# The within-chunk inverses of a chunked DeltaNet scan: stored transposes and joined 128-row products in place of transposes and 64-row products

## The chip, the cores and the metric

The kernel runs on one core of a Trainium2 chip. The metric is the device time of one execution in microseconds (us). The profile's engine names are used: PE is the matrix engine, PEld its weight loads, DVE the vector engine, ACT the scalar engine, POOL the GpSimd engine, SP the engine that issues most DMAs.

## The reference

One layer of a hybrid trunk over 2048 latent tokens and 256 context tokens of width 1024. A combined input projection feeds two token mixers: a bidirectional chunked gated DeltaNet (4 heads, key and value width 128, chunks of 64) and a windowed attention. Both are gated, projected, merged and projected again. The change touches the DeltaNet alone:

```python
a_mat = jnp.where(strict, einsum('nbhik,nbhjk->nbhij', kb, kc) * decay, 0.0)
t_mat = triangular_solve(a_mat, eye, lower=True, unit_diagonal=True)   # 64 x 64, one per chunk and head
u = einsum('nbhij,nbhjv->nbhiv', t_mat, vc * bc)
w = einsum('nbhij,nbhjk->nbhik', t_mat, kb * exp(gc))
...
v_new = u_n - w_n @ s                                  # one step of the scan over chunks
s_new = s * exp(gl_n) + kd_n.T @ v_new
o = qd_n @ s + qk_n @ v_new
...
o = o_f + rev(o_b)                                     # the same on the reversed sequence
```

## The kernel before, in words

The kernel works on blocks of 128 tokens, that is two of the reference's chunks: 2 context blocks and 16 latent ones, NC = 18. A block's 128x128 unit-triangular inverse is made of two 64x64 inverses on its diagonal and one off-diagonal 64x64 piece, which is minus (inverse) x (off-diagonal of the matrix) x (inverse).

Stages in order. First the norms, the state projection, the qkv projection with the short convolution; `finish` (from L591) forms the 128x128 key products of each block and `spill_blocks` (from L583) stores their diagonal 64x64 blocks in `Nsp` and the off-diagonal block in `offsp`. Then `base` (from L727) inverts the 64x64 blocks, 128 of them at a time with one block in each partition, by 62 pairs of DVE instructions (L758, L760): it runs twice, first for 8 chunks of each direction (si = 0), then for 8 more (si = 1), and stores the inverses in `Xset`. `base4` (from L775) does the last 2 chunks of each direction in another layout, as a generator whose pieces are placed among the steps of the scan; it stores `X4sp` in quarters. While `base` runs, PE does the gate projections (`gates`, `rest_run`, from L823: rps, L535 to L537 as recorded inside `fm_dense`).

Then the scan: 18 steps, each with one block forwards and one backwards. `chain` (from L1094) carries the state: ksps (L1109), vps (L1115), sps (L1127) on PE, x (L1102) on POOL, L1111, L1118 and L1133 on DVE, v2 (L1123) on ACT. `output` forms aps (L1151) and ops (L1162). `merge` (from L999) builds the two 128x128 inverses `mw` (forward, transposed, as vps needs it as its left operand) and `mx` (backward) for the next step: it loads the 64x64 inverses into zeroed tiles, transposes them on PE (L1027, L1029), copies (L1034, L1035), multiplies with the off-diagonal block (L1037 forward, L1039 backward; `in_step` issues the two directions alternately on different 64x64 parts of the PE array), evicts (L1041, L1042), multiplies again (L1044, L1046) and evicts into the off-diagonal quarter (L1048, L1049). `finalize` normalizes a block's output and transposes it (fps, L1078).

A planner orders each engine's instructions ahead of time from a simulated run, with priorities: the scan has the higher priority, and the gate projections of the other tokens (30 runs of 24 products before the attention is called for, 18 more behind it) fill PE between its steps. The attention follows (sc, L926 and on), and then the projections. At run time each engine, and SP's queue of DMAs, goes through its list in that fixed order.

Of the kernel before, what the change touches and what calls it, by code (L numbers as in the profile page):

```python
# [20 lines left out]
H = 4  # L21
# [19 lines left out]
def _hybrid(ctx, tc, nc, V, S, G, T, ins, out, dbg, upto):  # L41
# [61 lines left out]
    Xsp = [{}, {}]  # L103
    X4sp = dscr("X4sp", [2, 2, 4, 8, 64, 16])
    gsp = dscr("gsp", [1, D])
    osp = many("osp", NB, [128, H * 128])
    zasp = many("zasp", 4, [4, 128, 512])
# [623 lines left out]
    def base(si, npool, pool, fr, bk):  # L731


        n = 8 * len(fr)
        h1 = max(32, n)
        N = npool.tile([128, 64, 64], F32, name="N")
        nb = npool.tile([128, 64], F32, name="nb")
        if n < h1:
            G.memset(N[0:h1], 0.0)
            G.memset(nb[0:h1], 0.0)  # L740
        for d, chunks in ((0, fr), (1, bk)):
            for i0, c, k in runs(chunks):
# [24 lines left out]
        V.memset(A.rearrange("p r c -> p (r c)")[:, ::65], 1.0)  # L767
        for d, chunks in ((0, fr), (1, bk)):
            p0 = d * h1
            dma(Xset[d][si].rearrange("c h b r j -> (c h b) (r j)"), N[p0:p0 + n].rearrange("p r j -> p (r j)"))  # L770
            for ci, c in enumerate(chunks):
                Xsp[d][c] = Xset[d][si][ci]
        yield 1

    def base4(fr, bk):  # L775
# [8 lines left out]
        G.memset(nc_, 1.0)  # L784
        for d, chunks in ((0, fr), (1, bk)):
            c, p0 = chunks[0], d * 16
            dma((nc_, nb)[d][p0:p0 + 16], brT[c:c + 2, d * 4:d * 4 + 4].rearrange("c h (b t) -> c (h b) t", b=2))
            dma(N[p0:p0 + 16], Nsp[d][c:c + 2].rearrange("c h b r i -> (c h b) r i"))
        G.memset(X, 0.0)
# [18 lines left out]
        for d, chunks in ((0, fr), (1, bk)):  # L808
            for ci, c in enumerate(chunks):
                for q in range(4):  # L810
                    p0 = q * 32 + d * 16 + ci * 8
                    dma(X4sp[d, ci, q], X[p0:p0 + 8])
        yield

    def rest(ev, m, by_act):
# [43 lines left out]
    with tc.tile_pool(name="gate", bufs=1, reuse_waits="tile") as gp:  # L859
        gates(list(range(24)), (2, 3), behind(4, mod_gate(gp, ones)), by_act=True)  # L860
    LAST = (LAT(14, 15), LAT(0, 1))
    for si, (fr, bk, np_) in enumerate((([0, 1] + LAT(*range(0, 6)), [0, 1] + LAT(*range(10, 16)), bs),
                                        (LAT(*range(6, 14)), LAT(*range(2, 10)), bs2))):
        with tc.issue_after(last_conv[0].ins):
            for _ in base(si, np_, bs2, fr, bk):
                pass
    last_base = base4(*LAST)
    next(last_base)
    mem("r1a")
# [117 lines left out]
            weighted(n, kv, qs[n], pr.pop(i))  # L987


    def in_step(products):  # L990

        first = None
        for h in range(H):
            for p in products:
                with tc.issue_after(first.ins) if first else nullcontext():
                    i = p(h)
                first = i

    def merge(pool, cs):  # L999

        hs = range(H)
        Xs, offs, tp = [], [], []
        for d, c in enumerate(cs):
            X = pool.tile([128, H, 128], F32, name=f"mx{d}", bufs=2)
            G.memset(X, 0.0)
            if c in LAST[d]:
                x4 = pool.tile([128, 4, H, 16], F32, name="x4")
                for b in range(2):  # L1010
                    bs_ = slice(b * 64, b * 64 + 64)
                    for q in range(4):
                        dma(x4[bs_, q], X4sp[d, LAST[d].index(c), q, b::2].rearrange("h r s -> r h s"))
                    G.tensor_copy(X[bs_, :, bs_].rearrange("p h (s q) -> p h s q", q=4),
                                  x4[bs_].rearrange("p q h s -> p h s q"))
            else:
                for b in range(2):
                    dma(X[b * 64:b * 64 + 64, :, b * 64:b * 64 + 64], Xsp[d][c][:, b].rearrange("h r c -> r h c"))
            off = pool.tile([128, H, 64], F32, name=f"moff{d}", bufs=2)
            dma(off[64:128], offsp[d][c])  # L1020
            Xs.append(X)
            offs.append(off)
        for d in range(2):
            tps = psum(f"mg{d}", [128, H, 128], name="mtp")
            for h in hs:
                if d == 0:
                    T.transpose(tps[:, h], Xs[0][:, h], ident)  # L1027
                else:
                    T.transpose(tps[:, h, 64:128], Xs[1][64:128, h], ident[64:128, 64:128])  # L1029
            tp.append(tps)  # L1030
        brb = [br[:, c, d * 4:d * 4 + 4].unsqueeze(2).to_broadcast([128, H, 64]) for d, c in enumerate(cs)]
        y0, y1 = offs[0], pool.tile([128, H, 64], F32, name="my1")
        W, X = pool.tile([128, H, 128], F32, name="mw", bufs=2), Xs[1]
        S.copy(W, tp[0])  # L1034
        V.tensor_tensor(y1[64:128], tp[1][64:128, :, 64:128], brb[1][64:128], op=ALU.mult)  # L1035
        yps = [psum(f"mg{d}", [128, H, 128], name="myp") for d in range(2)]
        in_step([lambda h: T.matmul(yps[0][0:64, h, 0:64], lhsT=offs[0][64:128, h], rhs=W[64:128, h, 64:128],  # L1037
                                    start=True, stop=True),
                 lambda h: T.matmul(yps[1][64:128, h, 0:64], lhsT=offs[1][64:128, h], rhs=y1[64:128, h],  # L1039
                                    start=True, stop=True)])  # L1040
        V.tensor_tensor(y0[0:64], yps[0][0:64, :, 0:64], brb[0][0:64], op=ALU.mult)  # L1041
        S.copy(y1[0:64], yps[1][64:128, :, 0:64])  # L1042
        eps_ = [psum(f"mg{d}", [128, H, 128], name="mep") for d in range(2)]
        in_step([lambda h: T.matmul(eps_[0][0:64, h, 0:64], lhsT=Xs[0][0:64, h, 0:64], rhs=y0[0:64, h],  # L1044
                                    start=True, stop=True),
                 lambda h: T.matmul(eps_[1][64:128, h, 0:64], lhsT=y1[0:64, h], rhs=X[0:64, h, 0:64],  # L1046
                                    start=True, stop=True)])
        S.activation(W[0:64, :, 64:128], eps_[0][0:64, :, 0:64], AF.Copy, scale=-1.0)  # L1048
        S.activation(X[64:128, :, 0:64], eps_[1][64:128, :, 0:64], AF.Copy, scale=-1.0)  # L1049
        return W, X  # L1050

    def scan_consts(pool):
# [30 lines left out]
    def scan(pool, pool2, cs, after):  # L1083
# [83 lines left out]
                dma(osp[b], oa.rearrange("p h d -> p (h d)"))  # L1167
                seen.add(b)

        W = merge(pool, [orders[d][0] for d in range(2)])  # L1170
        for st in range(NC):
            r = [chain(d, st, W[d]) for d in range(2)]
            ready = [finalize(pool2, b, oa, cs, d) for b, oa, d in late]
            late.clear()
            if st + 1 < NC:
                W = merge(pool, [orders[d][st + 1] for d in range(2)])
            for rest in ready:
                rest()
            for d in range(2):
# [422 lines left out]
```

## Time and profile before

| what | value |
|---|---|
| three runs, us | 1989.85, 1990.79, 1998.35; median 1990.79 |
| the profiled execution, us | 1992.9, its span 1991.2 |
| mean granted clock of PE | 0.989 |
| PE, PEld busy | 1917.4 us (96%), 1605.6 us (81%) |
| DVE, ACT, POOL busy | 1502.1 us (75%), 802.6 us (40%), 692.1 us (35%) |
| DMA traffic | 333.12 MB, 387703 packets |

In the views, a row of a group gives line, engine, operation, destination and sources by tile name, shapes and count, then the busy time in us and the mean of one in ns, then the engine's idle time before it. A row of the timeline gives the start in us, the duration in us of the merged instructions, and what they are. Matmuls overlap in their pipeline, so what one costs PE is read from start to start, not from its duration. A float32 product appears as two matmul instructions. A row of stretches gives the stretch, its length, and then each engine's busy time with the number of instructions, the granted clock, the DMA engines' busy share and GB/s.

### The profile page before, as it was taken

The numbers are of one execution on the slowest core, as the hardware profiler recorded it, in microseconds if no ns is written. First come the engines' busy times: TensorE is split into PE (matmuls) and PEld (weight loads), VectorE is DVE, ScalarE is ACT, GpSimd is POOL, SyncE is SP. The second block draws the span as 40 slices with busy tenths as digits, with TensorE's granted clock in tenths as the row PEclk, the third lists the DMA queues.
The fourth block names the chain that finished last, engine by engine and source line by source line (L and its number), as shares of the span: only waits on it lengthen the run. The fifth ranks groups of instructions, "written<-read, shape, count | busy, mean of one in ns | idle before, by whom it ended". The sixth has DMA issues, their size and how long they took to land. (4 is left out here: it accounts for less than half of the span.)

```text
span 1991.2 us, 32088 instructions
## 1 busy us (share of the span) xinstructions
PE 1917.4 (96%) x10947; PEld 1605.6 (81%) x10947; DVE 1502.1 (75%) x2869; ACT 802.6 (40%) x1994; POOL 692.1 (35%) x768
## 2 busy tenths in 40 slices
PE   7999999989999999999999999999989999999998
PEld 4888888779998787877888888788778887877786
DVE  6979766668776999999677776536686878747888
ACT  5755545554443323111222233225665656532221
POOL 2742211235542202004222234323555443420675
PEclk9999999999999999999999999999999999999999
DMA  7552226765547633528977877674455655455454
GB/s 263 173 142 87 91 89 161 195 157 175 151 134 196 170 106 116 145 89 237 230 232 225 240 212 207 178 216 146 143 176 171 185 161 164 119 173 190 141 169 135
DMA packets 387703, 333.12 MB, mean 167 GB/s; under 512 B 83992, under 2 KB 307536, under 8 KB 386900
## 3 DMA queue, kind: packets, MB, share of 16 engines
q1 hardware_dynamic: 352244, 288.60, 50.1%
q10 hardware_dynamic: 35296, 42.48, 6.1%
q8 instruction: 87, 1.43, 0.3%
q14 instruction: 76, 0.62, 0.1%
HBM read 220.28 MB, written 109.13 MB: 165 GB/s over the span
## 5 line engine op out<-in xcount | busy, mean ns | idle before, releaser
L535 PE MATMUL rps<-hh,wh 128*128 128x512 f32 x768 | 309.3, 403 | 3.7 <-DVE rt L829 2.5
L537 PE MATMUL rps<-hh,wl 128*128 128x512 f32 x768 | 307.6, 401 | 0.0
L536 PE MATMUL rps<-hl,wh 128*128 128x512 f32 x768 | 307.5, 400 | 0.0
L574 DVE SCALAR_TENSOR_TENSOR cacc<-y,cw,cacc 128x512 f32<-128x512 f32 (+1 forms) x224 | 164.0, 752 | 22.2 <-ACT cacc L572 18.3
L535 PEld LDWEIGHTS rps<-hh,wh 128*128 128x128 f32 x768 | 145.3, 189 | 39.4 <-DVE rt L829 3.3
L535 PE MATMUL lps<-hh,wh 128*128 128x512 f32 (+1 forms) x448 | 171.8, 384 | 0.3 <-ACT y L645 0.3
L536 PE MATMUL lps<-hl,wh 128*128 128x512 f32 (+1 forms) x448 | 171.5, 383 | 0.0
L537 PEld LDWEIGHTS rps<-hh,wl 128*128 128x128 f32 x768 | 145.2, 189 | 32.6
L536 PEld LDWEIGHTS rps<-hl,wh 128*128 128x128 f32 x768 | 145.5, 189 | 31.9
L537 PE MATMUL lps<-hh,wl 128*128 128x512 f32 (+1 forms) x448 | 171.0, 382 | 0.0
L961 DVE TENSOR_TENSOR pl<-pt,ph 128x512 fp32r<-128x512 f32 x156 | 105.4, 685 | 42.9 <-ACT ph L959 42.1
L959 ACT CAST ph<-pt 128x512 fp32r<-128x512 f32 x156 | 90.2, 585 | 110.2 <-PE pt L957 77.0
L827 ACT ACTIVATE rt<-rps 128x512 f32<-128x512 f32 x96 | 57.3, 597 | 185.0 <-PE rps L537 169.0
L933 DVE CUSTOM_DVE_ANT_0 pr<-sc,band,sk 128x640 f32<-128x640 f32 (+1 forms) x128 | 106.6, 862 | 32.1 <-PE sc L929 16.2
L943 POOL TENSOR_SCALAR pr<-pr,sm 128x640 f32<-128x640 f32 (+1 forms) x128 | 99.7, 802 | 56.5 <-DVE sm L941 39.3
L760 DVE TENSOR_TENSOR N<-N,btmp 128x62 f32<-128x62 f32 (+30 forms) x124 | 116.7, 941 | 3.0
L758 DVE TENSOR_TENSOR btmp<-N 128x62 f32<-128x62 f32 (+30 forms) x124 | 116.4, 939 | 3.1
L935 ACT ACTIVATE pr<-pr,sm 128x640 f32<-128x640 f32 (+1 forms) x128 | 104.0, 815 | 20.5 <-DVE sm L933 20.4
L246 DVE TENSOR_TENSOR wl<-wr,wh 128x512 fp32r<-128x512 f32 x120 | 92.4, 783 | 24.4 <-POOL wh L245 22.1
L1247 PE MATMUL pps<-yh,wph 128*128 128x512 f32 x256 | 105.6, 414 | 4.7 <-DVE tb L1258 2.5
L245 POOL TENSOR_SCALAR wh<-wr 128x512 fp32r<-128x512 f32 x72 | 48.8, 692 | 169.8 <-PE lps L536 97.1
L1248 PE MATMUL pps<-yl,wph 128*128 128x512 f32 x256 | 101.8, 399 | 0.0
(378 smaller groups left out, 5025.4 us busy)
## 6 DMA issues: line engine op xcount, KB each, us to landing
wr<-in_w_in_dram SPq DMA_DIRECT2D x120, 256.0 KB
kw<-Ksp SPq DMA_DIRECT2D x28, 384.0 KB
x<-vsp SPq DMA_DIRECT2D x36, 256.0 KB
k<-ksp SPq DMA_DIRECT2D x34, 256.0 KB
kT<-kTsp SPq DMA_DIRECT2D x34, 256.0 KB
wm<-in_w_mod_dram SPq DMA_DIRECT2D x16, 512.0 KB
xt<-in_x_dram SPq DMA_DIRECT2D x16, 512.0 KB
dtl<-Dsp SPq DMA_DIRECT2D x32, 256.0 KB
```

Of the source, the lines that this page charges most:

```text
L535: T.matmul(ps, lhsT=wh[:, k], rhs=xh[:, k], start=k == 0, stop=False)
L536: T.matmul(ps, lhsT=wh[:, k], rhs=xl[:, k], start=False, stop=False)
L537: T.matmul(ps, lhsT=wl[:, k], rhs=xh[:, k], start=False, stop=k == kt - 1)
L574: V.scalar_tensor_tensor(a, y[:, t:t + n], cw[:, m, t:t + 1], a, op0=ALU.mult, op1=ALU.add)
L758: V.tensor_tensor(tv, A[:, m + 1:, m].unsqueeze(2).to_broadcast([h1 + n, r, m]), A[:, m, 0:m].unsqueeze(1).to_broadcast([h1 + n, r, m]), o ...
L760: V.tensor_tensor(A[:, m + 1:, 0:m], A[:, m + 1:, 0:m], tv, op=ALU.add)
L933: V.tensor_tensor_reduce(s_, ps[:, o:768], band[:, b0:b0 + W + 256], -0.125, sk[:, 1, hd:hd + 1], ALU.add, ALU.min, sm[:, h, 1:2])
L935: S.activation(s_, s_, AF.Exp, scale=-1.0, bias=sm[:, h, 1:2], accum_out=sm[:, h, 2:3])
L943: G.tensor_scalar(p[:, h, :W + 256], p[:, h, :W + 256], sm[:, h, 3:4], 1.0, op0=ALU.mult, op1=ALU.mult)
L961: V.tensor_tensor(pl, pt, f32(ph), op=ALU.subtract)
L1247: T.matmul(ps, lhsT=wh[:, k, ms], rhs=hs[k], start=k == 0, stop=False)
L1248: T.matmul(ps, lhsT=wh[:, k, ms], rhs=ls[k], start=False, stop=False)
```

## The change

`base` also copies each set of inverses transposed (four ACT copies of a quarter each, each followed by two stores to the new scratch `XTset`), and `base4` likewise (one ACT copy, 16 stores to `XT4sp`). `spill_blocks` stores the forward off-diagonal block from the untransposed product instead of the transposed one. `merge` loads the forward inverses transposed, places the off-diagonal blocks of the two directions in the two off-diagonal quarters of one 128x128 tile `off` that was zeroed once, and forms both directions' products in one product of 128 rows a head. The right-hand factors are stacked: `r1` is scaled by br on POOL before the first product, `r2` is copied by ACT. The transposes, DVE's two instructions and `in_step` are gone. The tiles are zeroed once (`merge_tiles`) and not in each step. `off` and the intermediate `z` have one buffer.

```diff
@@ spill_blocks
-        dma(offsp[d][c0:c0 + nn, :, h].rearrange("c r i -> r c i"), t[64:128, :, 0:64])
+        if d:
+            dma(offsp[1][c0:c0 + nn, :, h].rearrange("c r i -> r c i"), t[64:128, :, 0:64])
+            dma(offsp[0][c0:c0 + nn, :, h].rearrange("c r i -> r c i"), t[0:64, :, 64:128])
@@ base, after the store to Xset
+        for q in range(4):
+            xt = (pool.tile([128, 1376], F32, name="btmp") if npool is pool else
+                  xtp.tile([128, 1024], F32, name="xt"))[0:h1 + n, 0:1024].rearrange("p (j r) -> p j r", r=64)
+            S.copy(xt, A[:, :, q * 16:q * 16 + 16].rearrange("p r j -> p j r"))
+            for d in range(2):
+                dma(XTset[d][si].rearrange("c h b j r -> (c h b) j r")[:, q * 16:q * 16 + 16], xt[d * h1:d * h1 + n])
@@ base4, after the stores to X4sp
+        S.copy(N[:, 0:16], X.rearrange("p r s -> p s r"))
+        for d, chunks in ((0, fr), (1, bk)):
+            for ci, c in enumerate(chunks):
+                for q in range(4):
+                    p0 = q * 32 + d * 16 + ci * 8
+                    dma(XT4sp[d][ci].rearrange("h b (s q) r -> (h b) s q r", q=4)[:, :, q], N[p0:p0 + 8, 0:16])
@@ merge: the new body (the old one is in the listing above)
+        lo_, hi_ = slice(0, 64), slice(64, 128)
+        W, X, off, z = tiles[0][st % 2], tiles[1][st % 2], tiles[2], tiles[3]
+        r1 = pool.tile([128, H, 64], F32, name="mr1", bufs=2)
+        r2 = pool.tile([128, H, 64], F32, name="mr2", bufs=2)
...
+        for b, bs_ in enumerate((lo_, hi_)):
+            dma(W[bs_, :, bs_], blk(XTsp[0][cs[0]][:, b]))
+            if cs[1] in LAST[1]:
+                quarters(X[bs_, :, bs_], 1, b)
+            else:
+                dma(X[bs_, :, bs_], blk(Xsp[1][cs[1]][:, b]))
+        if cs[0] in LAST[0]:
+            quarters(r1[lo_], 0, 0)
+        else:
+            dma(r1[lo_], blk(Xsp[0][cs[0]][:, 0]))
+        dma(r1[hi_], blk(XTsp[1][cs[1]][:, 1]))
+        for d, (rows, cols) in enumerate(((lo_, hi_), (hi_, lo_))):
+            dma(off[rows, :, cols], offsp[d][cs[d]])
+            G.tensor_tensor(r1[rows], r1[rows], br[rows, cs[d], d * 4:d * 4 + 4].unsqueeze(2).to_broadcast([64, H, 64]),
+                            op=ALU.mult)
+        S.copy(r2[hi_], W[hi_, :, hi_])
+        S.copy(r2[lo_], X[lo_, :, lo_])
+        zps = psum("mg0", [128, H, 64], name="mzp")
         for h in range(H):
+            T.matmul(zps[:, h], lhsT=off[:, h], rhs=r1[:, h], start=True, stop=True)
+        S.copy(z[hi_, :, lo_], zps[hi_])
+        S.copy(z[lo_, :, hi_], zps[lo_])
+        eps_ = psum("mg1", [128, H, 64], name="mep")
+        for h in range(H):
+            T.matmul(eps_[:, h], lhsT=z[:, h], rhs=r2[:, h], start=True, stop=True)
+        S.activation(W[lo_, :, hi_], eps_[lo_], AF.Copy, scale=-1.0)
+        S.activation(X[hi_, :, lo_], eps_[hi_], AF.Copy, scale=-1.0)
         return W, X
```

In the steps whose blocks come from `base4` (the last two), `quarters` gathers an inverse from `X4sp` by four loads and a POOL copy, as the old code did.

More of the change, by code (lines that the diff above doesn't have):

```diff
@@ L102, in _hybrid @@
     Xset = [many(f"Xsp{d}_", 2, [8, H, 2, 64, 64]) for d in range(2)]
-    Xsp = [{}, {}]
+    XTset = [many(f"XTsp{d}_", 2, [8, H, 2, 64, 64]) for d in range(2)]
+    Xsp, XTsp = [{}, {}], [{}, {}]
     X4sp = dscr("X4sp", [2, 2, 4, 8, 64, 16])
+    XT4sp = many("XT4sp", 2, [2, H, 2, 64, 64])
     gsp = dscr("gsp", [1, D])
@@ L786, in base4 @@
             c, p0 = chunks[0], d * 16
+            for ci, c_ in enumerate(chunks):
+                XTsp[d][c_] = XT4sp[d][ci]
             dma((nc_, nb)[d][p0:p0 + 16], brT[c:c + 2, d * 4:d * 4 + 4].rearrange("c h (b t) -> c (h b) t", b=2))
@@ L861, in _hybrid @@
     LAST = (LAT(14, 15), LAT(0, 1))
+    xtp_ = tc.tile_pool(name="xtp", bufs=1, reuse_waits="tile")
+    xtp = xtp_.__enter__()
     for si, (fr, bk, np_) in enumerate((([0, 1] + LAT(*range(0, 6)), [0, 1] + LAT(*range(10, 16)), bs),
@@ L987, in attention @@
             weighted(n, kv, qs[n], pr.pop(i))
-    def in_step(products):
-        first = None
-        for h in range(H):
[L994 to L1049, printed above, removed]
@@ L1168, in output @@
                 seen.add(b)
-        W = merge(pool, [orders[d][0] for d in range(2)])
+        tiles = merge_tiles(pool)
+        W = merge(pool, [orders[d][0] for d in range(2)], 0, tiles)
         for st in range(NC):
@@ L1175, in scan @@
             if st + 1 < NC:
-                W = merge(pool, [orders[d][st + 1] for d in range(2)])
+                W = merge(pool, [orders[d][st + 1] for d in range(2)], st + 1, tiles)
             for rest in ready:
```

16 lines of the change are left out of this document (15 added, 1 removed).

## The prediction

> **What bounds the kernel now.** I read the page's first part, then PE stretch by stretch, then the groups, waits and timeline of the scan.
>
> ```profile
> PE 1917.4 (96%) x10947; PEld 1605.6 (81%) x10947; DVE 1502.1 (75%) x2869; ACT 802.6 (40%) x1994; POOL 692.1 (35%) x768
> 650.00:890.00 240.00, 237.48 (x1006) 188.81 (x1004) 229.36 (x265) 57.21 (x98) 29.85 (x23) 0.99 0.44 126
> 890.00:1320.00 430.00, 421.39 (x3017) 364.80 (x3017) 308.41 (x718) 109.31 (x357) 141.53 (x218) 0.99 0.75 215
> 1342.00:1765.00 423.00, 407.51 (x2207) 340.74 (x2206) 303.54 (x649) 242.93 (x526) 193.74 (x204) 1.00 0.50 156
> ```
>
> The stretches are the inversions (650 to 890), the scan (890 to 1320) and the attention. In the scan PE is without work for only 430.0 - 421.4 = 8.6 us, at a full clock; DVE has 122 us free, ACT 321 and POOL 288. So the scan lasts as long as PE's instructions do: its own and the gate products between its steps. These are the shares (after the bar busy us and mean ns):
>
> ```profile
> L535 PE MATMUL rps<-hh,wh 128*128 128x512 f32 x300 | 123.0, 410 | 0.1
> L1027 PE MATMUL mtp<-ident,mx 128*128 128x128 f32 x72 | 12.6, 272 | 0.0
> L1029 PE MATMUL mtp<-ident,mx 64*128 64x64 f32 x72 | 8.3, 235 | 0.0
> L1037 PE MATMUL myp<-mw,moff 64*64 64x64 f32 x144 | 13.4, 226 | 0.0
> PE mep L1044 <- DVE moff L1041: 1.5, 1, 1.5
> PE ksps L1109 <- DVE S L1133: 4.2, 2, 4.0
> ```
>
> Gate work reaches past the end of the scan: the gate weights' last split on DVE starts at 1381.7, the attention's first score matmul at 1342.6 (third number after the colon is the longest duration, then the first and last start):
>
> ```profile
> L246 DVE TENSOR_TENSOR wl<-wr,wh x120: 673/684/1782, 132.0 to 1381.7; 128x512 fp32r<-128x512 f32 x120
> L926 PE MATMUL sc<-kw,qT x128: 278/354/523, 1342.6 to 1738.4; 128*128 128x384 f32 x112, 128*128 128x256 f32 x16
> ```
>
> So a scan that ends up to some 39 us later leaves PE with work until the attention begins. That cover I use below.
>
> **The change on PE.** What an instruction costs PE is the distance of starts, which the timeline shows.
>
> ```profile
> 1084.27 1.05 PE L1115 MATMUL vps<-x,mw 128*128 128x128 f32 x8
> 1085.16 0.38 PE L1027 MATMUL mtp<-ident,mx 128*128 128x128 f32 x2
> 1085.38 0.83 PE L1151 MATMUL aps<-S,qT 128*128 128x128 f32 x6
> ...
> 1072.41 1.95 PE L1127 MATMUL sps<-v,k 128*128 128x128 f32 x16
> 1074.29 0.27 PE L1037 MATMUL myp<-mw,moff 64*64 64x64 f32 x1
> 1074.30 0.27 PE L1039 MATMUL myp<-my,moff 64*64 64x64 f32 x1
> 1074.40 0.22 PE L1037 MATMUL myp<-mw,moff 64*64 64x64 f32 x1
> ...
> 1074.75 0.22 PE L1039 MATMUL myp<-my,moff 64*64 64x64 f32 x1
> 1074.90 1.16 PE L1151 MATMUL aps<-S,qT 128*128 128x128 f32 x8
> 1087.17 0.38 PE L1027 MATMUL mtp<-ident,mx 128*128 128x128 f32 x2
> 1087.48 0.46 PE L1029 MATMUL mtp<-ident,mx 64*128 64x64 f32 x4
> 1087.87 0.50 PE L537 MATMUL rps<-hh,wl 128*128 128x512 f32 x1
> ```
>
> A full 128-row matmul costs (1085.16 - 1084.27) / 8 = 0.111 us, a 128-row transpose 0.22 / 2 = 0.11. The block of 16 small matmuls: sps, 16 at 0.111, would hand over at 1074.19, and the next full matmul starts at 1074.90, so the block costs 0.71, of which 0.10 goes at its start and 0.15 behind its last start. The four small transposes: two L1027 end their turn at 1087.39, rps starts at 1087.87, so 0.48.
>
> Before, a step costs 4 x 0.11 + 0.48 + 2 x 0.71 = 2.34 us, in 18 steps 42.1 us. The counts agree (72 = 18 x 4, 144 = 18 x 8).
>
> After, a step has two products of four heads, each head two matmuls: 16 with a 128x128 left operand and 64 moving columns. No row has this shape. Its price lies between the small pairs, (1074.75 - 1074.40) / 6 = 0.058 a pair from the second pair to the eighth, and the full 0.111. Two rows tell which end is near:
>
> ```profile
> 20.98 1.94 PE L328 MATMUL mtp<-sel,mrow 4*128 4x2 f32 x16
> 441.12 0.56 PE L546 MATMUL gps<-g,mats 128*128 128x72 f32 x4
> 441.62 0.50 PE L535 MATMUL lps<-hh,wh 128*128 128x512 f32 x1
> ```
>
> L328 moves only two columns against 128-column weights, and its 16 still stand (1.94 - 0.27) / 15 = 0.111 apart or more (0.27, the last one's own duration, is that of the longest small matmul above). L546, with 72 columns, hands over after 0.50 / 4 = 0.125. So loading 128 float32 columns sets the pace, and I take 0.111: 16 x 0.111 = 1.78 a step, 32.0 us in 18. PE gains 42.1 - 32.0 = 10.1 us. At 0.058 it would gain 25.4.
>
> Here a rule speaks against the change. The Trainium skill (TensorE: Matmul & The Clock Gate, Part 3: Packing small matmuls) says that operands narrower than the array leave it idle and should be packed as tiles that run side by side. The kernel before does that. By the rule the products alone go from 2 x 0.71 to 1.78 a step, 6.5 us worse in 18 steps, and with the waits taken below the time would be about 1999. The rows agree with the rule as to the products (0.058 a pair); the transposes, 0.92 a step, and the 0.25 us at the block's two ends turn the balance.
>
> The wait of L1044 for L1041 (1.5 us) goes with that instruction. Late next is z: PE's second product then waits for two ACT copies instead of a DVE and an ACT one. The sum takes the gain of 1.5.
>
> **The change on the other engines.**
>
> ```profile
> L1034 ACT COPY mw<-mtp 128x512 f32<-128x512 f32 x18 | 10.8, 600 | 7.5 <-PE mtp L1027 7.4
> L1042 ACT COPY my<-myp 64x256 f32<-64x256 f32 x18 | 6.6, 369 | 72.0 <-PE myp L1039 68.1 <-DVE wl L246 3.9
> L1035 DVE TENSOR_TENSOR my<-mtp,br 64x256 f32<-64x256 f32 x18 | 7.7, 428 | 5.4 <-PE mtp L1029 4.9
> L1102 POOL TENSOR_TENSOR x<-x,rin 128x512 f32<-128x512 f32 x36 | 42.6, 1187 | 39.0 <-DMA x<-vsp 31.2 <-DVE N L795 7.7
> L1007 POOL MEMSET mx<- 128x512 f32 x36 | 18.8, 527 | 67.8 <-ACT fjunk L1066 22.1 <-issue 18.1 <-PE mep L1046 16.1
> POOL qd L1147 <- DMA qd<-QDsp: 99.2, 27, 8.3
> ```
>
> DVE loses L1035 and L1041, which is of the same shape, 2 x 0.43 a step, 15 us in all; with 122 us free that is worth nothing but shorter waits. ACT loses one 0.600 and one 0.369 copy a step and gets four of 0.369: +0.5 a step, 9 us, into 321 free. POOL loses two memsets (1.05) and gets two multiplications over 256 columns, half of L1102's 512, so about 0.59 each: +0.14 a step, and 6 memsets (3.2 us) once. In busy time these cost nothing; in full uncovered they would be 9 + 2.5 + 3 us. But each multiplication waits for a load, and behind it in POOL's queue stand x (L1102), the mask of qd and the gate weights' conversion. That is the rival.
>
> The transposed stores: nine ACT copies of 128 x 1024, two L1034 each, 1.2 us, 11 us in all (22 if the strided read halves the rate), 16 stores of 256 KB, 16 of 32 KB. The first set runs under gate products in a stretch where ACT has 183 of 240 us free and the DMA share is 0.44. The second set falls at about 953 to 985, in the scan. It has a single buffer, so each copy waits for the store before, and SP's queue, with the scan's loads behind, waits for each copy; base4 reloads its tile after the last. If the cover is gone there, four round trips of about 4 us cost 16 us once.
>
> ```profile
> DMA packets 124745, 92.32 MB, mean 215 GB/s; under 512 B 31962, under 2 KB 102300, under 8 KB 124445
> q1 hardware_dynamic: 121533, 85.99, 70.8%
> 1230.59 0.43 SPq L1106 DMA_DIRECT2D kT<-kTsp  x1
> 1231.07 2.65 SPq L812 DMA_DIRECT2D X4sp<-btmp  x6
> 1235.39 4.68 SPq L1013 DMA_DIRECT2D x<-X4sp  x6
> ```
>
> The scan's loads: per step four of inverses and two of off become eight pieces, all in rows of 256 B (off had 1 KB), so 1152 packets become 2048, 16 thousand more in all and 2.4 MB. q1's packets take 70.8% of 16 engines for 430 us, 40 ns for a mean one, or 57 ns per KB: between 2.4 MB x 57 / 16 = 8 us and 16 thousand x 40 / 16 = 40 us of the 16 engines' time, 2 to 9 points on 0.75. It stays below 1, and I price it with the waits. base4's 16 further stores take some 0.45 us each of SP (L812), 7 us, ahead of the loads of the last two steps (L1013), which themselves become 12 quarters from 16. Lateness there is covered by the gate products up to the 39 us above. spill_blocks moves a source, nothing else: no cost, no cover needed.
>
> For all new waits together (POOL, SP, the single buffers of off and z) the bounds are -7, if PE's other 7.1 us of idle time in the scan went as DVE gets freer, and +18, one us a step. The waits that now reach PE in 430 us sum to under 9 us although POOL stands 99 us waiting for qd alone, so I take a small part of the upper end, +3.
>
> **Sum.** -10.1 - 1.5 + 3 = -8.6 us. The profiled execution took 1992.9, 2.1 above the median of 1990.79; from it the sum gives 1984.3, and referred to the median 1982.2. I forecast 1982.
>
> **The rivals.**
>
> Gain larger, 1970: the moving columns set the pace after all (0.058, another -15), or the freer DVE takes PE's idle time (-7). For it: DVE is in PE's waits. Against: L328. The Trainium skill (TensorE: Matmul & The Clock Gate, Back-to-back issue gap) gives some 81 ns a matmul for 128 columns in a steady stream; the trace's 111 differs, and decides; by 81 ns the new products would cost 23.3 us and the estimate from that page is 1973.
>
> Nothing moves, 1990: the gain on PE comes, and as much is lost where fixed orders, made from a simulated run, meet later loads (the 953 to 985 stretch, or the attention, in which PE has 15.5 us without work and which then starts with less gate work beside it). For it: DMA at 0.75. Against: PE's few waits.
>
> Slower, 2010: POOL's queue. The 36 new multiplications stand behind loads; x now waits 31.2 us in 18 waits, 1.7 each. If such a wait a step goes through x to vps and PE, 18 x 1.7 = 31 us come on top of -11.6: 2010. It decides from 0.64 us a step. For it: POOL does wait for DMAs in most steps. Against: 288 us of slack, and gate products between x and vps.
>
> **How the numbers follow.** Forecast 0.50, larger gain 0.15, nothing 0.20, slower 0.15. The forecast's own range is 1976 to 1989 (waits -3 to +10). For 8 in 10 I cut the ends of both outer rivals: 1970 to 2002. About 0.5%, 10 us, is what a measurement of this kernel can tell from no change, so faster is below 1981 and slower above 2001. The forecast splits 0.23 faster and 0.27 same; larger gain is faster; nothing gives 0.17 same and 0.03 slower; slower gives 0.12 and 0.03 same. Together 0.38, 0.47, 0.15.
>
> **What would show it.** 288 matmuls at 0.111 us from start to start in place of 720; no L1027 to L1046 transposes; PE idle in the scan still near 9 us; ACT's copies at about 1.2 us under full PE; DMA share of the scan at 0.77 to 0.84. The prediction is wrong if the new matmuls run near 0.058, if PE shows waits for POOL or ACT at the two new products or at x, or if the stretch around 960 or the end of the scan has gaps on PE.

## The result, and the profile after

The changed kernel is slower by 1.4%: median 2022.17 us of 4 runs (2018.04 to 2026.32) against 1994.57 of 4 for the kernel before, a ratio of 1.0137 with a 95% interval of 1.0097 to 1.0176. The profiled execution took 2021.38 us, its span 2019.7. The forecast was 1982 us, with a range of 1970 to 2002.

PE has less to do and stands longer. The page's first part of the changed kernel:

```profile
PE 1913.1 (95%) x10515; PEld 1606.0 (80%) x10515; DVE 1485.0 (74%) x2833; ACT 830.5 (41%) x2039; POOL 696.1 (34%) x772
```

PE is busy 4.3 us less than before, yet idle for 2019.7 - 1913.1 = 106.6 us, against 1991.2 - 1917.4 = 73.8 before. Where, is read from stretches of the whole span. First the kernel before, then the changed one; the third number is PE's busy time, the last three the granted clock, the DMA share and GB/s:

```profile
890.00:1050.00 160.00, 157.50 (x1087) 133.89 (x1087) 130.29 (x261) 32.34 (x84) 51.40 (x70) 0.99 0.82 229
1200.00:1400.00 200.00, 193.68 (x1195) 165.79 (x1194) 104.83 (x255) 68.58 (x215) 68.65 (x112) 0.98 0.61 179
```

```profile
890.00:1050.00 160.00, 143.07 (x772) 119.96 (x771) 103.09 (x181) 45.53 (x84) 52.26 (x70) 0.96 0.83 221
1200.00:1400.00 200.00, 181.50 (x1075) 157.15 (x1075) 97.46 (x247) 61.81 (x218) 60.90 (x110) 0.97 0.70 203
```

At the scan's start PE works 157.50 - 143.07 = 14.4 us less, and at its end 12.2 less. Between them (1050 to 1200) it idles 1.3 us against 0.8. The 4.5 us more of idle time before 890 are also there in s2 (table below), whose code up to 890 is the old one, so they are not put down to the change.

**The new products cost what was forecast.** In the middle of the scan the timeline of PE shows one step's two products and what starts behind them:

```profile
1092.17 1.00 PE L1058 MATMUL mep<-mr,mz 128*128 128x64 f32 x8
1092.99 0.48 PE L537 MATMUL rps<-hh,wh 128*128 128x512 f32 x1
...
1118.82 1.00 PE L1053 MATMUL mzp<-mr,moff 128*128 128x64 f32 x8
1119.66 1.11 PE L1173 MATMUL ops<-v,qd 128*128 128x128 f32 x8
```

From start to start that is 0.82 + 0.84 = 1.66 us a step, against 1.78 forecast and 2.34 in the kernel before.

**The start.** The first set's four transposed copies run at the scan's start. The first two in ACT's timeline (idle time and what ended it in brackets):

```profile
896.54 2.09 ACT L780 COPY xt<-N 128x1024 f32<-128x1024 f32 x1 [0.40 <-PE gsum L229]
903.10 2.10 ACT L780 COPY xt<-N 128x1024 f32<-128x1024 f32 x1 [4.47 <-DMA XTsp<-xt]
```

The inverses were stored at 809.8. The copies wait 87 us more, for gsum, a product of the gates' stage: the pool of `xt` is opened where the gates' pool has just closed, takes over its memory, and gsum is the last to read there. The scan's first vps comes at 951.1 and not at 920.9.

From 890 to 1050 PE stops for these (us in all, times, longest), and two of the stops stand behind them as the timeline has them:

```profile
PE aps L1162 <- DVE oa L1174: 6.8, 2, 3.6
PE mzp L1053 <- ACT rt L845: 4.3, 1, 4.3
PE mzp L1053 <- DMA moff<-offsp: 2.5, 4, 0.8
PE mzp L1053 <- POOL mr L1047: 1.8, 1, 1.8
PE sps L1138 <- ACT v L1134: 1.4, 1, 1.4
```

```profile
955.44 1.08 PE L1053 MATMUL mzp<-mr,moff 128*128 128x64 f32 x8 [0.81 <-DMA moff<-offsp]
981.32 1.94 PE L1053 MATMUL mzp<-mr,moff 128*128 128x64 f32 x8 [4.28 <-ACT rt L845]
```

Half of it, 8.6 of 16.8 us, is at the merge's first product. The longest of these stops is put down to ACT, but off's two loads, which this product reads, landed only at 980.8 and 981.1: without ACT it would have been shorter by 0.3 us at most. Another 6.8 us are two waits of aps for DVE, and they come by another way:

```profile
1020.06 3.02 DVE L807 TENSOR_TENSOR N<-N,btmp 32x256 f32<-32x256 f32 x4 [9.35 <-DMA wr<-in_w_in_dram]
1042.39 0.26 DVE L815 TENSOR_TENSOR btmp<-N,btmp 128x63 f32<-128x63 f32 x1 [6.83 <-DMA N<-N]
```

```profile
1025.27 0.49 PE L1162 MATMUL aps<-S,qT 128*128 128x128 f32 x2 [3.19 <-DVE oa L1174]
1043.59 1.63 PE L1162 MATMUL aps<-S,qT 128*128 128x128 f32 x8 [3.58 <-DVE oa L1174]
```

L807 and L815 are among the first steps of `base4` (the profile puts the first wait to a load of weights, but L807 reads `base4`'s own tiles), and in DVE's fixed order they stand ahead of the scan's oa. `base4` loads its matrices into the tile that the second set's transposed copies have just read, so these loads are issued at 1009.7 and not, as in the kernel before, at 965.6. DVE stands for them, and PE for DVE. This is read from one trace; no run tests it alone.

The DMA issues from 920 to 1060 tell what the queue carried, first before, then after:

```profile
x<-vsp SPq DMA_DIRECT2D x14, 256.0 KB
```

```profile
x<-vsp SPq DMA_DIRECT2D x10, 256.0 KB
XTsp<-btmp SPq DMA_DIRECT2D x8, 256.0 KB
moff<-offsp SPq DMA_DIRECT2D x17, 64.0 KB
XTsp<-xt SPq DMA_DIRECT2D x4, 256.0 KB
```

At nearly the same DMA share and rate (0.82 and 0.83, 229 and 221 GB/s in the stretches from 890 to 1050), 3 MB of stores went through, and the loads of two steps fewer (two of x a step).

**The end.** SP's timeline at the scan's end, cut to the weight loads (L243) and the first and last of base4's new stores (L830); behind it PE's timeline, cut to its two longest stops, and one stretch:

```profile
1247.24 0.46 SPq L243 DMA_DIRECT2D wr<-in_w_in_dram  x1
...
1266.01 0.78 SPq L830 DMA_DIRECT2D XT4sp<-N  x1
...
1313.55 0.66 SPq L830 DMA_DIRECT2D XT4sp<-N  x1
1314.26 1.48 SPq L243 DMA_DIRECT2D wr<-in_w_in_dram  x2
```

```profile
1275.49 1.45 PE L1138 MATMUL sps<-v,k 128*128 128x128 f32 x8 [4.58 <-ACT v L1134]
...
1319.16 0.80 PE L537 MATMUL rps<-hh,wh 128*128 128x512 f32 x1 [7.43 <-POOL wh L247]
```

```profile
1310.00:1320.00 10.00, 2.57 (x14) 2.09 (x13) 2.59 (x6) 0.60 (x1) 5.41 (x11) 0.69 0.68 186
```

For 67 us no gate weight is loaded. The last is used up, and PE waits 7.43 us for the next to be loaded and converted. The granted clock is 0.69 on average in that stretch (0.50 from 1313.8 to 1323.9). The Trainium skill (TensorE: Matmul & The Clock Gate, HAM oscillation) has it that idle gaps of PE over some 3.4 us throttle it again; this row agrees, but shorter stops were followed by the same here: in the kernel before, behind a stop of 1.47 us that ended at 978.6, the clock was 0.50 from 979.8 to 983.1. So a stop costs more than its own length.

### The profile page after: what moved, and what is told of

It is laid out like the page before. It is cut to its first block, busy times and chain, and to the rows that moved or that the text cites. A ratio compares the mean times of both kernels' runs of the same rounds, so it can differ in the third digit from the quotient of the medians.

```text
span 2019.7 us, 31250 instructions
## 1 busy us (share of the span) xinstructions
PE 1913.1 (95%) x10515; PEld 1606.0 (80%) x10515; DVE 1485.0 (74%) x2833; ACT 830.5 (41%) x2039; POOL 696.1 (34%) x772
## 5 line engine op out<-in xcount | busy, mean ns | idle before, releaser
L537 PE MATMUL rps<-hh,wh 128*128 128x512 f32 x768 | 310.7, 405 | 15.8 <-POOL wh L247 7.4
L954 DVE CUSTOM_DVE_ANT_0 pr<-sc,band,sk 128x640 f32<-128x640 f32 (+1 forms) x128 | 106.6, 862 | 18.4 <-PE sc L950 13.4
```

Source lines behind the costliest of these rows:

```text
L537: T.matmul(ps, lhsT=wh[:, k], rhs=xh[:, k], start=k == 0, stop=False)
L954: V.tensor_tensor_reduce(s_, ps[:, o:768], band[:, b0:b0 + W + 256], -0.125, sk[:, 1, hd:hd + 1], ALU.add, ALU.min, sm[:, h, 1:2])
```

## The experiments

One table holds them all: the ratio to the kernel before on the same chip (interval), and PE's idle time in us of the profiled execution by stretch (length less busy time, as above; "1400-end" reaches to the span's end). The profiled execution is one of several and lies up to 9 us from the median (w2 below it, s3 above it). The table leaves out PE's busy time, which moves too: for the same 10515 matmuls it is 1909 us in e4 and d1 (mean granted clock 0.988), 1913 in the changed kernel (0.985) and 1923 in e1 and e3 (0.984 and 0.982).

| kernel | median us | ratio | 0-890 | 890-1050 | 1050-1200 | 1200-1400 | 1400-end |
|---|---|---|---|---|---|---|---|
| before | 1994.57 | 1 | 31.2 | 2.5 | 0.8 | 6.3 | 33.0 |
| after | 2022.17 | 1.0137 (1.0097-1.0176) | 35.7 | 16.9 | 1.3 | 18.5 | 34.1 |
| e1 | 2031.04 | 1.0190 (1.0158-1.0221) | 35.9 | 22.2 | 9.5 | 5.3 | 32.1 |
| e2 | 2016.48 | 1.0109 (1.0078-1.0141) | 35.9 | 13.6 | 0.6 | 11.4 | 29.6 |
| e3 | 2038.28 | 1.0233 (1.0199-1.0268) | 43.8 | 19.9 | 10.2 | 12.6 | 28.8 |
| e4 | 2010.30 | 1.0091 (1.0059-1.0123) | 36.0 | 15.8 | 1.1 | 10.3 | 30.5 |
| w1 | 2015.98 | 1.0130 (1.0108-1.0153) | 39.3 | 12.6 | 0.1 | 13.3 | 34.6 |
| w2 | 2028.06 | 1.0186 (1.0149-1.0223) | 36.5 | 14.7 | 0.2 | 19.6 | 32.8 |
| w3 | 1996.28 | 1.0023 (1.0004-1.0042) | 34.7 | 1.9 | 0.0 | 5.4 | 32.8 |
| w4 | 2039.49 | 1.0245 (1.0223-1.0267) | 44.7 | 11.9 | 7.8 | 19.1 | 32.5 |
| o1 | 2024.20 | 1.0175 (1.0138-1.0212) | 36.2 | 16.0 | 0.6 | 18.1 | 35.2 |
| o2 | 2019.76 | 1.0153 (1.0130-1.0175) | 36.4 | 14.6 | 1.3 | 18.5 | 33.6 |
| o3 | 2017.69 | 1.0141 (1.0117-1.0166) | 35.0 | 19.5 | 0.0 | 11.8 | 36.6 |
| o4 | 2026.31 | 1.0181 (1.0156-1.0207) | 37.5 | 19.2 | 11.1 | 6.3 | 31.3 |
| s1 | 2015.77 | 1.0143 (1.0124-1.0161) | 36.3 | 12.6 | 1.9 | 17.4 | 31.6 |
| s2 | 2004.21 | 1.0090 (1.0071-1.0110) | 37.0 | 7.7 | 0.3 | 2.6 | 33.0 |
| s3 | 2018.06 | 1.0166 (1.0140-1.0192) | 38.0 | 23.9 | 7.0 | 6.8 | 29.5 |
| s4 | 2024.17 | 1.0182 (1.0159-1.0205) | 38.9 | 25.7 | 7.8 | 6.6 | 29.4 |
| d1 | 2006.51 | 1.0098 (1.0063-1.0134) | 36.1 | 18.3 | 1.0 | 7.2 | 34.6 |
| d2 | 2027.88 | 1.0217 (1.0177-1.0256) | 35.6 | 16.6 | 1.1 | 19.4 | 34.0 |

### The halves of the change, and two of its places

Theory A: the stores and where they fall cost the time. Rival, Theory B: the new merge does.

e1, the new merge without transposed copies and stores (it reads untransposed inverses in their place, so its values are not the reference's):

```diff
-        for q in range(4):
-            xt = ...; S.copy(xt, ...); dma(XTset[d][si]..., xt[...])
-                Xsp[d][c], XTsp[d][c] = Xset[d][si][ci], XTset[d][si][ci]
+                Xsp[d][c], XTsp[d][c] = Xset[d][si][ci], Xset[d][si][ci]
-        S.copy(N[:, 0:16], X...); dma(XT4sp...)      # base4, likewise
```

> The changed kernel without any of the transposed copies and stores (both sets of base and base4 leave them out; merge's loads of a transposed inverse read the untransposed one in the same shape, so the values differ and the loads do not). Theory A, the stores and their places cost the time and the new merge brings PE's 10 us: 1978 to 1990, PE's idle time in the scan near 10 us. Theory B, the new merge itself costs (POOL's multiplications behind loads, single buffers of off and z, two more loads a step): 2012 to 2025, with PE waiting in most steps.

e2, the old merge (and old `spill_blocks`) with the copies and stores, which nothing reads:

> The kernel before with the transposed copies and stores added and nothing reading them; merge is the old one. Theory A: 2022 to 2040, since the stores' cost is there and PE's 10 us are not gained; but where the scan does not wait for these stores, as nothing reads them here, less of it shows (then 2000 to 2015). Theory B: within 8 us of before, 1987 to 2003.

e3, the changed kernel with memory of its own for the first set's copies; to make room, a weight buffer of the gates' stage goes from two to one:

```diff
-                wm = pool.tile(..., name="wmg", bufs=2)
+                wm = pool.tile(..., name="wmg", bufs=1)
-    xtp = tc.tile_pool(name="xtp", ...)              # behind the gates' pool
+    xtp = tc.tile_pool(name="xtp", ...)              # ahead of the gates' pool
-        for q in range(4): ... [128, 1024] ...
+        for q in range(8 for the first set): ... [128, 512] ...
```

> The changed kernel with the buffer of the first set's transposed copies in memory of its own (half the size, 8 copies in place of 4; the gate's weight buffer has one copy in place of two to make room). The trace of the changed kernel has the first copy at 896.5, let go by gsum of the gate job at 895.9, 87 us after the set itself was stored. Theory A1, this wait is what makes the scan start late and the loss is mostly this: the copies at about 810 to 845, the first vps near 921, 1995 to 2008. Theory A2, the second set's copies and base4's stores carry the loss: 2015 to 2024, with the copies early all the same.

e4, the changed kernel without base4's transposed copy and its 16 stores (the last two steps read other inverses, so their values are not the reference's):

> The changed kernel without base4's transposed copy and 16 stores (the last two steps read the first set's inverses in their place, so the values differ). Theory A3, the end of the scan waits for these stores (16 stores between 1266 and 1314 in the changed kernel, PE idle some 14 us from 1270 to 1320): 2005 to 2013. If the end is covered by gate products: 2016 to 2024.

Neither A nor B holds alone: the new merge alone loses 1.9%, the stores alone 1.1%, both 1.4%. Both cost in the same stretch, the scan's start, and don't add; e1 and e2 lie outside the ranges of both theories. In e3 the scan begins 16 us earlier, and the kernel is slower than the changed one, outside both of its ranges. That speaks against the late start as the main cost, but it doesn't settle it: e3 also idles 8 us more before 890, and no gate product runs in it from 950 to 1025 (as in e1, below). e4 goes as expected. One of its stretches, and the same of the changed kernel behind it:

```profile
1300.00:1350.00 50.00, 49.25 (x306) 43.11 (x305) 25.57 (x61) 16.22 (x65) 14.74 (x31) 1.00 0.58 170
```

```profile
1300.00:1350.00 50.00, 42.52 (x253) 37.14 (x252) 20.96 (x46) 12.68 (x45) 15.24 (x28) 0.90 0.57 154
```

6.7 us of PE come back in 1300 to 1350, and the wait of 7.43 us for the next gate weight is gone. The intervals of the two ratios overlap, but the other runs agree: with base4's stores on SP's queue PE idles 18 to 20 us from 1200 to 1400 (in e2 and e3 11 to 13), without them 3 to 13. A wait of 4.9 to 8.2 us for a gate weight stands there in seven of the eight kernels that have these stores on SP's queue (all but e3), and in none of the others. Issued by ACT they cost as much in s1 (17.4, PE then waits for ACT) and less in o3 and s4.

### Is it the missing filling?

Why is e1 the slower half? The stretches of e1 for the gate products alone (rps) show it; those of the kernel before and of w1 stand behind:

```profile
950.00:975.00 25.00, 0.00 (x0) 0.00 (x0) 0.00 (x0) 0.00 (x0) 0.93 0.88 224
975.00:1000.00 25.00, 0.00 (x0) 0.00 (x0) 0.00 (x0) 0.00 (x0) 1.00 1.08 284
1000.00:1025.00 25.00, 0.00 (x0) 0.00 (x0) 0.00 (x0) 0.00 (x0) 0.86 1.01 266
```

```profile
950.00:975.00 25.00, 14.88 (x59) 10.41 (x58) 1.36 (x2) 1.20 (x2) 1.00 1.01 234
975.00:1000.00 25.00, 13.77 (x51) 9.89 (x50) 1.36 (x2) 1.20 (x2) 0.93 0.94 263
```

```profile
950.00:975.00 25.00, 11.38 (x43) 8.12 (x43) 2.73 (x4) 2.39 (x4) 0.93 0.87 227
975.00:1000.00 25.00, 15.11 (x52) 11.00 (x53) 1.36 (x2) 1.20 (x2) 0.86 0.95 241
```

No weight load is issued from 900 to 1050: the shorter merge lets the planner go on with the scan, whose loads have priority, and the gate weights' loads come behind them. On the chip the DMA engines are then full (1.08, 1.01) and PE has nothing beside the scan. Theory C: this filling is what is lost. Four runs give the weights' loads the scan's priority: w1 in e1, w2 in the changed kernel, w3 in the kernel before, w4 in e3.

```diff
-        w = weights(w_in[:, ...], KT, by_act)
+        with tc.high_priority(0 if by_act or m >= BESIDE else tc.cur_priority):
+            w = weights(w_in[:, ...], KT, by_act)
```

> The new merge alone (no transposed copies or stores; it reads the untransposed sets, so the inverses it forms are not the reference's), with one thing added: the loads and conversions of the gate products' weights get the scan's priority in the planned order. Theory C (the new merge gives PE less to wait for, the scan's loads then come thick on SP's queue, the weight loads of the gate products are ordered behind them, and PE stands without its filling: in the run of the new merge alone no weight load is issued from 900 to 1050 us and no gate product runs from 930 to 1040): 1985 to 2000 us, and 25 to 40 gate products of each of three kinds in every 25 us from 925 on. Theory B (the new merge itself costs, by its loads, POOL's multiplication or the single buffers): 2020 to 2040 us, as without the priority.

> The changed kernel, complete, with the weight loads of the gate products at the scan's priority. Theory C: the gate products are already spread over most of its steps, so only a part comes back, where two stretches of 25 us had no weight load (about 1255 to 1305): 2008 to 2022 us; the scan still starts 27 us late and its tail still waits for base4's stores. Theory B: 2018 to 2030 us.

> The kernel before with the weight loads of the gate products at the scan's priority: the control. Theory C: its gate products are spread already, so within 10 us of the kernel before, 1984 to 2002 us. If the priority itself gains (that is, if it is not the missing filling that it mends in the new merge), well below 1984.

> The changed kernel with memory of its own for the first set's transposed copies (in eight parts, as in the earlier run) and the weight loads at the scan's priority; the computation is complete. Theory C (the early start alone was slower because the scan ran without the gate products): 1990 to 2012 us, below the same start without the priority by 25 to 45 us and below the changed kernel. Theory B: 2030 to 2045 us, as without the priority.

C holds for a part of e1: w1 has the filling back and gains 0.6%, some 12 us (the intervals are just apart), but is still 1.3% slower than before, between the ranges of its two theories. In the changed kernel (w2) and in the early start (w4) the priority gains nothing. In w4 gate products run in every 25 us of the start, the scan begins 13 us earlier than in the changed kernel, and still PE idles 11.9 us from 890 to 1050 and 7.8 to 1200. At w2's end the pause in the weight loads is still there, from 1239 to 1318 us. w3 says that a newly planned order by itself does no such harm: it idles 1.9 us at the start.

### Is it off's load?

Theory D: PE stops at mzp because off's load comes last and off has one buffer. o1 puts off's loads first, o2 does so and gives off two buffers (and r1 and r2 one), o3 is o1 with the transposed stores issued by ACT, o4 is e1 with off's loads first.

```diff
+        for d, (rows, cols) in enumerate(((lo_, hi_), (hi_, lo_))):
+            dma(off[rows, :, cols], offsp[d][cs[d]])      # o1: ahead of the inverses
-    "moff", "mz"   ->   "moff0", "moff1", "mz"            # o2
-                dma(XTset[d][si]...)   ->   adma(...)     # o3, XT4sp likewise
```

> The changed kernel, complete, with one thing moved: the two loads of off, the last of a merge's loads on SP's queue, are put first. PE's planned order is the same as the changed kernel's, product for product. Theory D (the new merge's first product needs the whole off tile, which has one buffer, so its load can only start when the step before has used it and then lands after PE has come to it: nearly every pause of PE from 940 to 1060 us in the changed kernel and in the new merge alone ends at this product): the pauses at that product shrink and the time falls to 2005 to 2015 us. Rival E (the loads are late because the 16 DMA engines are full then, whichever is issued first): within 5 us of the changed kernel, 2017 to 2027 us.

> The changed kernel, complete, with off in two buffers (r1 and r2 give one of theirs for the memory) and off's loads first. Theory D: no wait for off is left, 2000 to 2012 us, less than with the loads moved alone. Rival E: 2015 to 2030 us.

> The changed kernel, complete, with off's loads first and the stores of the transposed copies issued by ACT behind its own copies and not by SP (SP's queue waited 9.6 us for those copies from 890 to 1050 us, with the scan's loads behind). Theory A (the stores and their places cost, by holding SP's queue): 1995 to 2010 us, below the variant with off's loads first alone. Theory E: no more than 5 us below it.

> The new merge alone (no transposed copies or stores; it reads the untransposed sets, so the inverses it forms are not the reference's), with off's loads first. In its planned order the gate products are spread over all steps again (14 to 50 a step, where the new merge alone had 0 in ten steps). Theory D and the missing filling together: 1990 to 2008 us. Rival E: 2012 to 2035 us.

None comes below 1.4% slower, so D as it stood falls. (o4 is no clean test: no gate product ran in it from 950 to 1025 either.) In o2 no wait for off is left, but PE then waits 9.1 us in 4 waits at the same product for POOL's r1, whose load has the single buffer now. o3 takes 6 us from the end (11.8 idle), and the start has 3.5 us more.

### Is it SP's queue?

Theory S: SP issues one DMA after another, mostly in 0.4 to 0.8 us each from 950 to 1050, and is the serial resource. Summed from the trace, its issuing took 0.88 of the stretch 950 to 1000 and 0.76 of 1000 to 1050 in the changed kernel, 0.77 and 0.56 before. s1 to s4 issue the merge's loads from ACT's queue: in the changed kernel, before, e1 and e3 (s1 and s4 the transposed stores too).

```diff
 def merge(...):
-            dma(W[bs_, :, bs_], ...)      # and every other load of merge
+            adma(W[bs_, :, bs_], ...)
```

> The changed kernel, complete, with the merge's loads and the stores of the transposed copies issued by ACT and not by SP (about 8 loads a step and 32 stores in all). Theory S (SP's queue is the serial resource: it spends 0.4 to 0.7 us on each DMA, and where that fills over 0.7 of a stretch every load behind comes late to PE): PE's idle time from 890 to 1050 us falls from 16.9 to 5 to 10 us, and from 1200 to 1400 from 18.5 to about 8; 1992 to 2006 us. Rival E (DMA engines full, or the loads' own latency): 2013 to 2027 us.

> The kernel before with the merge's loads issued by ACT: the control. Its PE idles 2.5 us from 890 to 1050 and 6.3 from 1200 to 1400, so Theory S gives it little: 1983 to 1998 us. Rival E: 1988 to 2000 us.

> The new merge alone (no transposed copies or stores; it reads the untransposed sets, so the inverses it forms are not the reference's), with the merge's loads issued by ACT. Its planned order has 13 to 57 gate products in every step. Theory S: 1985 to 2003 us, against 2031 with SP's queue. Rival E: 2015 to 2035 us.

> The changed kernel, complete, with memory of its own for the first set's transposed copies (in eight parts), and the merge's loads and the transposed stores issued by ACT. Theory S: the early start now pays, 1990 to 2010 us. Rival E: 2030 to 2042 us, as in both earlier runs with the early start.

SP's share fell to 0.35 and 0.41 in s1, and the kernel stayed 1.4% slower: S falls as the cause. The Trainium skill (DMA: Bandwidth & Descriptors, Issuing engines are not separate DMA queues) says that DMAs of all issuing engines end on the same 16 engines, and that issuing from several saves the sequencer's time alone; s1 agrees. None of the four gained measurably on the kernel that it starts from: s3 and s4 are 0.2% and 0.5% below e1 and e3, with overlapping intervals. The control s2 lost 0.9%, at 2004 us above both of its ranges. So the old merge too pays when the place of its loads is changed.

### Is it the lead of the loads?

How long before its use a load is issued: off's loads on SP's queue and the first product with them, first the changed kernel's fifth merge (two loads; the product that needs them stands above, at 981.32), then the fourth of the kernel before with its first product from PE's timeline:

```profile
976.11 1.25 SPq L1046 DMA_DIRECT2D moff<-offsp  x2
```

```profile
937.89 0.47 SPq L1020 DMA_DIRECT2D moff<-offsp  x1
...
968.39 0.27 PE L1037 MATMUL myp<-mw,moff 64*64 64x64 f32 x1
```

From the last issue to the first product it is 15, 20, 24, 30, 37 us in the first five steps before, and 5.3, 3.0, 3.9, 4.6, 4.1, 5.5 in steps 2 to 7 of the changed kernel; in w1 such a load took 4.0 us to land (median of the three from 920 to 1060 whose landing the trace tells). In the steady part the changed kernel has 14 to 18 us and doesn't stop. Theory L: this lead is what the new merge loses. The old merge had two buffers for off and needed it only for its second kind of product, behind the transposes. d1 gives every loaded tile of w1 two buffers with off's loads first, d2 the same buffers in the changed kernel.

```diff
-    "moff", "mz"                                   ->  "moff0", "moff1", "mz"
-    r2 = pool.tile(..., name="mr2", bufs=2)        ->  bufs=1
```

> The new merge alone (no transposed copies or stores; it reads the untransposed sets, so the inverses it forms are not the reference's), with two buffers for each tile that a merge loads (off too; the copied r2 gives one of its two for the memory), off's loads first and the weight loads at the scan's priority, which spreads the gate products over all steps. Theory L (what the new merge loses is the lead of its loads, by the single buffer of off and by needing all its loads in its first product): PE's idle time from 890 to 1050 us falls from 12.6 (with the weight loads first alone) to below 6; 1990 to 2004 us against 2016. Rival E (the loads are late in that stretch because the DMA engines are full, whatever their buffers): 2010 to 2030 us.

> The changed kernel, complete, with two buffers for each tile that a merge loads (r2 one). Theory L: the pauses at the merge's first product from 940 to 1060 us shrink, but the transposed copies and stores keep the scan's start late and its end waiting, so idle time from 890 to 1050 us falls from 16.9 to about 10 and the time to 2010 to 2018 us. Rival E: 2018 to 2026 us.

d1 is the fastest of the runs with the new merge alone, 2006.5, and by the ratios 0.9% below e1, with the intervals apart. But it misses its 1990 to 2004 us, and at the scan's start PE idles more than in w1, 18.3 us against 12.6, where below 6 were expected; what it gains on w1 is at the scan's end (7.2 us against 13.3). PE's waits from 890 to 1050, w1 and then d1:

```profile
PE mzp L1042 <- DMA moff<-offsp: 5.9, 3, 2.5
PE mep L1047 <- ACT mr L1038: 4.7, 1, 4.7
PE mzp L1042 <- POOL qd L1147: 2.0, 1, 2.0
```

```profile
PE sps L1128 <- DVE rt L836: 5.2, 1, 5.2
PE aps L1152 <- DVE S L1134: 3.9, 1, 3.9
PE ksps L1110 <- DMA kT<-kTsp: 3.4, 1, 3.4
PE mzp L1043 <- DMA mx<-Xsp: 2.5, 1, 2.5
```

The wait for off is gone (its lead is 5 to 20 us in steps 1 to 6 of d1), and other late inputs stand in its place; by the ratios d1 is 0.3% below w1, with overlapping intervals. d2 gains nothing, against an expected 2010 to 2018 us, so L as it stood falls too.

**What is shown and what stays open.** Shown: each half of the change slows the kernel alone; the end's loss goes largely with base4's stores, ahead of the gate weights; of the new merge's own loss some 12 us are the missing filling. Not settled: what makes up the rest at the start. Waits for off, r1, r2, kT and DVE each came up where another was removed, in a stretch with the DMA share at 0.8 to 1.08. Loads that come late because those engines are full (rival E) would look so, and half of the times fell into E's ranges. But a full share alone doesn't stop PE: from 950 to 1000 it was 0.98 in the kernel before, which idled 1.5 us there, and 0.86 in the changed kernel, which idled 6.0. No run took traffic out of that stretch without changing the order too. No kernel with the new merge or the stores comes down to the time of the kernel before.

## Why the prediction was wrong

The term of PE was right: 1.66 us a step measured, 1.78 taken. The Trainium skill's rule on packing (TensorE: Matmul & The Clock Gate, Part 3: Packing small matmuls) held for the products alone, as the forecast said (1.66 against 2 x 0.71), and the transposes turned the balance on PE (2.34 before). PE's busy time fell by only 4.3 us and not by 18 x (2.34 - 1.66) = 12.2. The mean granted clock was 0.985 and not 0.989, an estimate of 1913 x 0.004 / 0.989 = 7.7 us of longer work, for which the forecast had no term; in d1, at 0.988, the busy time fell by 1917.4 - 1909.0 = 8.4.

**The step that failed** is the +3 us "for all new waits together", bounded by +18 as one us a step. Measured: 14.4 us at the scan's start and 12.2 at its end, 26.6, with next to nothing in the steps between. I averaged over steps a cost that sits in two stretches. Three statements under it did not carry:

- "The first set runs under gate products": a tile takes its place in memory from a closed pool, and the copies waited for that pool's last reader, to 896.5 us. (That this lateness is itself a main cost, the early starts e3, w4 and s4 do not show.) I looked at ACT's free time and not at the memory.
- "Lateness there is covered by the gate products up to the 39 us": the cover needs its own weights, and they stood on the same SP queue behind the 16 stores that I had priced at 7 us of SP (11.1 us measured). A cover fed by the queue that is late is no cover.
- "It stays below 1": so it did, 0.79 from 890 to 1320. But it says nothing of whether a load comes in time. In the kernel before it was 0.98 from 950 to 1000, where off was loaded 15 to 37 us ahead and PE hardly stopped. I quoted the average of 430 us and did not look at the lead.

The four round trips of the second set, priced at 16 us once if uncovered and then left out of the sum, came about: ACT waited 17.3 us for them in three waits, and `base4`'s loads, DVE and PE came late behind them (6.8 us of PE, above). ACT's nine copies took 2.0 to 2.1 us each and not 1.2, 18.3 us in all, nearer the 22 that I named as the other end than the 11.

The rival "nothing moves" had the mechanism, fixed orders that meet later loads, and in part the place (953 to 985, where 5.6 us of the start's 16.9 lie); it took about 10 us for it, a third. The rival of POOL's queue did not happen: x waited longer for its loads (60.1 us against 31.2), but PE waited for POOL's multiplication 1.8 us in the scan. "Larger gain" was excluded by the price of the products.

## What to carry to other kernels

Before calling work hidden, follow what feeds the work that hides it: its loads stand on some queue, and if the change adds to that queue, cover and covered are late together. Look at the DMA share and at the lead of loads (issue to first use) in the stretch where a phase begins, not on average: a lead that falls from 15 to 37 us to about the 4 us that a load takes is a stall in waiting. And where an order is planned ahead, a shorter dependency chain lets the planner take the filling away from where it was needed; count the filling products per stretch in the new order.

## What the runs showed of the hardware

- Two groups of the changed kernel: a transposing copy of 128x1024 on ACT, read with a stride, takes 1.7 times as long as two contiguous 128x512 copies (0.600 us each in L1034 of the kernel before, which read PE's results and not a tile in memory).

```profile
L780 ACT COPY xt<-N 128x1024 f32<-128x1024 f32 x4 | 8.4, 2091 | 15.4 <-DMA XTsp<-xt 15.0 <-PE gsum L229 0.4
L780 ACT COPY btmp<-N 128x1024 f32<-128x1024 f32 x4 | 7.9, 1983 | 20.7 <-DMA XTsp<-btmp 17.3 <-DVE N L771 3.4
```

- A load of 64 KB in rows of 256 B holds SP as long as one of 256 KB or longer: 0.57 to 0.61 us (off, the inverses) against 0.42 (k) and 0.55 (x), medians of the changed kernel from 890 to 1350.
- Eight float32 matmuls of 128x128 weights hand over after 0.82 to 0.84 us with 64 moving columns, as fast as those with 128 (0.111 us each) to within 8%: half the moving columns save next to nothing.
- PE's granted clock was 0.50 for 3.4 us behind a stop of only 1.47 us (kernel before, 979.8 to 983.1), and in that time eight 128x128 matmuls of aps took 1.66 us, against 1.06 at full clock.
